# Head norms by transposes and a VectorE sum, and a new order of steps, in a two-layer RWKV-7 and dilated-attention trunk

## The chip, the cores and the metric

One core of a Trainium2 chip runs the whole program. The metric is the device time of one execution in microseconds, the median of several runs. The granted clock of TensorE, which rows below show, has two levels, 1.2 and 2.4 GHz (0.50 and 1.00 in the rows).

## The reference, cut to what matters

The trunk has two layers on 512 positions of width 1024. Each is a feed-forward block, a mixer, and a second feed-forward block. The first mixer is an RWKV-7 scan with 12 heads of 64 plus attention to a memory of 256 rows; the second is dilated attention in 12 heads plus attention to the same memory. The change concerns the norms over the 64 columns of a head:

```python
kk = split_heads(k * kk_scale)
kk = kk / jnp.maximum(jnp.linalg.norm(kk, axis=-1, keepdims=True), 1e-12)   # RWKV keys
...
var = jnp.mean(jnp.square(y - mean), axis=-1, keepdims=True)                # RWKV output
y = ((y - mean) * lax.rsqrt(var + LNX_EPS)).reshape(b, s, RWKV_W) * lnx_g + lnx_b
...
k = rms_norm(split_heads(k), k_gain)        # shared keys of the second mixer
q = rms_norm(q, q_gain)                     # queries of both mixers
```

## The kernel before, in words

Everything is held transposed: a tile `[128, 512]` has two heads of 64 channels on the partitions and the 512 positions along the row. The four feed-forward blocks (tile `fps` in PSUM) and the projections of the mixers (tiles `mm`) multiply in three passes: a value is split into a high and a low part (`uh`, `ul`, `whi`, `wlo`), and each product is three matmuls of 512 columns.

A mixer is a set of generators ("strands"). `weave` runs them in one thread of program order: each letter of `ORDER_A` or `ORDER_B` takes one step of one strand, and a step whose condition doesn't hold yet is owed and taken as soon as it can. In mixer A the letters are a: `finish` (the recurrence and the output norm of a pair of heads), b and c: `scan` of even and odd pairs (the triangular solve), d: `prepare`, e and f: the memory attention of two head pairs, g: the projections, h: the first part of the output projection. In mixer B they are a: memory attention, b and c: dilated attention of even and odd units, d: `settle` (norms of queries and keys, transposes of values), e: projections, f: the first part of the output projection. Each engine works through its own queue in program order.

The norm of a head needs the sum of 64 squares that lie on 64 partitions. ScalarE squares the tile into `sq`. `roots` then takes four blocks of 128 positions as the stationary operand and multiplies each by `pair`, two columns of ones and zeros; the result in a `sc` bank is `[128 positions, 4 blocks, 2 heads]`. VectorE scales it and takes the reciprocal, ScalarE takes the square root, in the wide form spread over 64 columns per head. `spread` brings it back to channels on partitions: four matmuls of 128 columns against the identity, into another `sc` bank, which VectorE multiplies into the tile. Queries of mixer B and of the memory attention need the root by position alone, and use no `spread`.

`roots` is called 14 times in each mixer: in A by `rwkv_prepare` (6), `rwkv_finish` (6) and the memory queries (2), in B for 6 key tiles and 8 query tiles. `spread` is called 12 times in A and 6 times in B. A reader of the profile meets all of this under the line of one recording helper, L309, so that groups are told apart by tile and shape: `sc<-cst,tmp` with `128x2` is `roots`, with `128x128` it is `spread` (and the transposes of values in `settle`).

Of the kernel before, what the change touches and what calls it, by code (L numbers as in the profile page):

```python
# [13 lines left out]
ALU = mybir.AluOpType  # L14
AX = mybir.AxisListType
PSUM = bass.MemoryType.PSUM

P = 128
# [5 lines left out]
HD = 64  # L24
# [143 lines left out]
def wide(t):  # L168
    return t.unsqueeze(1).broadcast_to([P, NCH, C])
# [14 lines left out]
class Operand:  # L184
# [40 lines left out]


ORDER_A = (
    "abcdeaefhhhhhhggggggggfgggggggggggggggggggggggggggggggggggggdddgddggggddddddggdgggggddbbbbbbbggggggb"
    "ddggbbggdbgggggbbgdbdgbbggddddbddggbbggggbggbbgeeeegbdgbbddgaacccaaccaaccgaagaagaacggagaccaaagggaacg"
    "gacchhhhgaaaagcddgdhhhhgccgggcdccdggcggddddddbbccgcggaaaaadcgddgcaggagaaagabbbbbgaaabgaaabbggaabgabg"  # L230
    "ggbgagaaabdbddbgggbgbbddbggddddddbgbbggbbgaadaagaagddgaacaaccaagaagcaaaccggggccaccgacaccggaaaagggcdd"
    "dccgcgccddbbgggcgdddddddccgcggccdgaadaagaagbaabaabbbaagaabgaaabbgaabaggbgggbgagaaagbdddbbgggbdccgbbg"
    "dgbddddddbffcfbbdbbaaddaaaaaacaacccecaaffaacceaaacfcecceeccfaaffecccaeceafaaaacffcchchcahaahaaaahaaa"
    "haaahaaahhaahhaahaahhhhhhhhhhhhhhhhhhhhh"
)
ORDER_B = (
    "ccccabdedfeeeeeeeeeeeeeeeeeeeddddeeddddeeeeeeeeeddddeebbeeebbeeeedaadeedeeddeeeeeddeeeedddeeeeeeedde"
    "edddeeeedeeeeddeeeeedddeeeeeeeedddecceebeeeeeeeeeeeeebddddbbbbbbbceccccccceeeadeedddeffffeeebaaabbee"
    "eeeeeeeacaaaadddcceeeeaedaaeeaeeeedddeeeeeaeaaeddddedddeeedddeeeeeededeedddeeeeeeddeedddbbbbeeeecccc"
    "eedddeeeeeeeeeeeeeeeebdddddcbbbbffccfbbbbcfcccfccffbbffbffcffcc"  # L240
)
WAIT, FREE = "wait", "free"

# [118 lines left out]
class Net:  # L362
# [37 lines left out]
    def load_constants(self):  # L400
        nc = self.nc
        width = self.ap["cst"].shape[1]
        t = self.cp.tile([P, width], F32, name="cst")
        nc.sync.dma_start(t, self.ap["cst"])
        off = 0
        for n, w in zip(CONST_N, CONST_W):
            setattr(self, n, t[:, off:off + w])
            off += w
        self.pair = self.same.rearrange("p (e u) -> p e u", e=2)[:, :, 0]

    def gain(self, i):
        return self.gains[:, i:i + 1]
# [157 lines left out]
    def roots(self, sq, n, bank, wide, keep, *change):  # L570

        nc, nb = self.nc, n // P
        ps = bank("sc")[:, :nb * 2].rearrange("p (b e) -> p b e", e=2)
        for b in range(nb):
            nc.tensor.matmul(ps[:, b], sq[:, b * P:(b + 1) * P], self.pair, start=True, stop=True,
                             skip_group_check=True)
        r = keep or self.cp.tile([P, 4, 2], F32, tag="roots", bufs=2, name=self.nm("roots"))[:, :nb]
        nc.vector.tensor_scalar(r, ps, *change[:2], **{f"op{i}": o for i, o in enumerate(change[2:])})
        nc.vector.reciprocal(r, r)
        yield WAIT  # L580
        if wide:
            w = wide().rearrange("p (b e u) -> p b e u", e=2, u=HD)
            nc.scalar.activation(w, r.unsqueeze(3).broadcast_to([P, nb, 2, HD]), AF.Sqrt)
            r = w.rearrange("p b e u -> p b (e u)")
        else:
            nc.scalar.activation(r, r, AF.Sqrt)
        yield WAIT
        return r

    def spread(self, r, ps):  # L590

        for b in range(r.shape[1]):
            self.nc.tensor.matmul(ps[:, b * P:(b + 1) * P], r[:, b], self.ident, start=True, stop=True,
                                  skip_group_check=True)

    def head_norm(self, out, t, gain, tmp, bank, n, wide=True):

# [761 lines left out]
```

## Time and profile before

| | us |
|---|---|
| median of 3 runs (lowest, highest) | 2098.99 (2094.82, 2103.91) |
| the profiled execution's own time | 2096.68 |
| its span, first to last instruction | 2094.9 |
| TensorE busy in the span | 2049.4 (98%) |
| VectorE, ScalarE, GpSimd busy | 860.6, 817.0, 588.4 |
| mean granted clock of TensorE | 0.992 |

Busy time of TensorE is the union of its matmuls; they are pipelined, so the distance from one start to the next tells more of a matmul's price than its duration. By the tiles, the mixer A has TensorE from 385.5 to 769.2 us of the span and mixer B from 1508.0 to 1729.2 us; the rest are feed-forward blocks.

### The profile page before, as it was taken

The page shows a single profiled execution, that of the slowest core. Times are in us where ns is not written, and L with a number is a line of the kernel's source. Part 1 is how long each engine was busy: PE and PEld are TensorE (multiplying, and loading weights), DVE is VectorE, ACT ScalarE, POOL GpSimd, SP SyncE. Part 2 cuts the span into 40 slices and gives each one's busy share as a digit, 9 for nine tenths or more (in the row PEclk, how much of TensorE's full clock was granted, in tenths as well). Part 3 has the DMA queues.
Part 4 walks back from the last instruction along what each step waited for, and adds up shares of the span by engine and source line. Part 5 has one row for each costly group of instructions (what it writes and reads, how often), then busy time and mean ns, then how long its engine had stood idle before and what let it go on. Part 6 is the DMA issues. An engine that isn't in the chain of part 4 may idle for free.

```text
span 2094.9 us, 35917 instructions
## 1 busy us (share of the span) xinstructions
PE 2049.4 (98%) x14594; PEld 1666.8 (80%) x14594; DVE 860.6 (41%) x1294; ACT 817.0 (39%) x1418; POOL 588.4 (28%) x513
## 2 busy tenths in 40 slices
PE   8999999999998899999999999999999989999999
PEld 6888888877776687788888888888787868888887
DVE  6333333455455355333434433333416375333322
ACT  6333333434334554333433433333336554333321
POOL 2222222553332152222222222222232224222221
PEclk9999999999999999999999999999999999999999
DMA  5333344411100173443344422334521154222342
GB/s 198 96 96 99 93 124 137 124 48 44 36 28 20 45 255 110 135 144 99 110 136 132 146 96 96 100 100 129 157 94 46 43 180 146 95 97 96 99 132 80
DMA packets 130645, 222.13 MB, mean 106 GB/s; under 512 B 14232, under 2 KB 31824, under 8 KB 130480
## 3 DMA queue, kind: packets, MB, share of 16 engines
q1 hardware_dynamic: 130480, 219.85, 33.6%
q8 instruction: 114, 1.87, 0.4%
q14 instruction: 51, 0.42, 0.1%
HBM read 202.90 MB, written 21.61 MB: 107 GB/s over the span
## 4 chain that ended last, share of the span: by engine, by line
PE 71%; DVE 2%; ACT 1%; issue 0%; DMA 0%; ACTq 0%; DVEq 0%
PE fps L309 52%; PE mm L309 10%; PE sc L309 8%; PE py L309 2%; ACT krv L309 0%; DVE prob L309 0%; DVE x L309 0%; DVE mx L309 0%; DVE dmx L309 0%; DVE ul L309 0%; DVE mpr L309 0%; ACT L309 0%; DVE tx L309 0%; ACT tmp L309 0%; DMA xd<-x 0%
## 5 line engine op out<-in xcount | busy, mean ns | idle before, releaser
L309 POOL TENSOR_TENSOR wlo<-raw,whi 128x512 fp32r<-128x512 f32 (+3 forms) x404 | 495.1, 1227 | 1369.8 <-ACT whi L309 1352.7
L309 ACT ACTIVATE whi<-raw 128x512 fp32r<-128x512 f32 (+3 forms) x684 | 415.6, 610 | 935.2 <-PE fps L309 780.2
L309 PE MATMUL fps<-uh,whi 128*128 128x512 f32 x1408 | 551.5, 392 | 8.0 <-ACT whi L309 8.0
L309 PE MATMUL fps<-uh,wlo 128*128 128x512 f32 x1408 | 549.5, 390 | 1.4 <-POOL wlo L309 1.0
L309 PE MATMUL fps<-ul,whi 128*128 128x512 f32 x1408 | 548.9, 390 | 0.0
L309 DVE TENSOR_TENSOR wlo<-raw,whi 128x512 fp32r<-128x512 f32 x280 | 200.8, 718 | 345.1 <-ACT whi L309 335.4
L309 PEld LDWEIGHTS fps<-uh,whi 128*128 128x128 f32 x1408 | 265.0, 188 | 67.5 <-ACT whi L309 12.3
L309 PEld LDWEIGHTS fps<-uh,wlo 128*128 128x128 f32 x1408 | 264.8, 188 | 58.7 <-POOL wlo L309 2.0
L309 PEld LDWEIGHTS fps<-ul,whi 128*128 128x128 f32 x1408 | 264.9, 188 | 55.7 <-issue 0.7
L309 PE MATMUL fps<-hh,whi 128*128 128x512 f32 x704 | 273.9, 389 | 0.0
L309 PE MATMUL fps<-hl,whi 128*128 128x512 f32 x704 | 273.9, 389 | 0.0
L309 PE MATMUL fps<-hh,wlo 128*128 128x512 f32 x704 | 273.9, 389 | 0.0
L309 DVE TENSOR_TENSOR gs<-fps,rstd 128x512 f32<-128x512 f32 x88 | 60.5, 690 | 322.5 <-PE fps L309 322.5
L309 PEld LDWEIGHTS fps<-hl,whi 128*128 128x128 f32 x704 | 132.2, 188 | 27.6
L309 PEld LDWEIGHTS fps<-hh,whi 128*128 128x128 f32 x704 | 132.2, 188 | 27.3
L309 PEld LDWEIGHTS fps<-hh,wlo 128*128 128x128 f32 x704 | 132.2, 188 | 27.3
L309 PE MATMUL mm<-uh,whi 128*128 128x512 f32 x280 | 125.0, 447 | 0.4 <-DVE p L309 0.2
L309 PE MATMUL mm<-uh,wlo 128*128 128x512 f32 x280 | 111.9, 399 | 0.0
L309 PE MATMUL mm<-ul,whi 128*128 128x512 f32 x280 | 111.6, 399 | 0.0
L309 DVE TENSOR_TENSOR hm<-fps,gs 128x512 f32<-128x512 f32 x88 | 60.6, 691 | 121.0 <-PE fps L309 115.8
L309 DVE TENSOR_TENSOR hl<-hm,hh 128x512 fp32r<-128x512 f32 x88 | 77.2, 880 | 50.7 <-ACT hh L309 50.6
L309 PEld LDWEIGHTS mm<-uh,whi 128*128 128x128 f32 x280 | 53.4, 191 | 17.3 <-issue 5.0
(260 smaller groups left out, 2025.6 us busy)
## 6 DMA issues: line engine op xcount, KB each, us to landing
raw<-w SPq DMA_DIRECT2D x512, 256.0 KB, 2.6
raw<-wa_in SPq DMA_DIRECT2D x44, 256.0 KB, 2.7
xd<-x SPq DMA_DIRECT2D x40, 256.0 KB, 3.4
tmp<-xd SPq DMA_DIRECT2D x32, 256.0 KB, 3.2
xin<-xd SPq DMA_DIRECT2D x32, 256.0 KB, 4.4
raw<-w_kv SPq DMA_DIRECT2D x24, 256.0 KB, 2.7
raw<-w SPq DMA_DIRECT2D x32, 128.0 KB, 2.4
raw<-wmem SPq DMA_DIRECT2D x16, 256.0 KB, 2.6
```

The source lines that it names most:

```text
L309: r = f(*args, **kw)
```

## The change

`roots` no longer multiplies the four blocks of squares by two columns. It transposes them on TensorE, so that a `sc` bank holds all 512 squares with positions on the partitions, and VectorE adds up 64 columns per head with a `tensor_reduce` from PSUM. The scaling is then a `tensor_scalar` of its own on the sums in SBUF. `spread` uses transposes in place of matmuls with the identity. `pair` goes. The two order strings are new; they hold the same number of letters of each kind, and the code of the strands is otherwise the same.

```diff
 ORDER_A = (
-    "abcdeaefhhhhhhggggggggfgggggggggggggggggggggggggggggggggggggdddgddggggddddddggdgggggddbbbbbbbggggggb"
...
+    "eeabcdafghhhhghhhhgggggggfgebbbbeeegggggggggggggggggggggggggggggggggggggdddgddggggddddddggbbbdgggggddg"
...
 ORDER_B = (
...
-        self.pair = self.same.rearrange("p (e u) -> p e u", e=2)[:, :, 0]
...
     def roots(self, sq, n, bank, wide, keep, *change):
         nc, nb = self.nc, n // P
-        ps = bank("sc")[:, :nb * 2].rearrange("p (b e) -> p b e", e=2)
+        ps = bank("sc")[:, :n].rearrange("p (b u) -> p b u", u=P)
         for b in range(nb):
-            nc.tensor.matmul(ps[:, b], sq[:, b * P:(b + 1) * P], self.pair, start=True, stop=True,
-                             skip_group_check=True)
+            nc.tensor.transpose(ps[:, b], sq[:, b * P:(b + 1) * P], self.ident)
         r = keep or self.cp.tile([P, 4, 2], F32, tag="roots", bufs=2, name=self.nm("roots"))[:, :nb]
-        nc.vector.tensor_scalar(r, ps, *change[:2], **{f"op{i}": o for i, o in enumerate(change[2:])})
+        nc.vector.tensor_reduce(r, ps.rearrange("p b (e u) -> p b e u", u=HD), axis=AX.X, op=ALU.add)
+        nc.vector.tensor_scalar(r, r, *change[:2], **{f"op{i}": o for i, o in enumerate(change[2:])})
         nc.vector.reciprocal(r, r)
...
     def spread(self, r, ps):
         for b in range(r.shape[1]):
-            self.nc.tensor.matmul(ps[:, b * P:(b + 1) * P], r[:, b], self.ident, start=True, stop=True,
-                                  skip_group_check=True)
+            self.nc.tensor.transpose(ps[:, b * P:(b + 1) * P], r[:, b], self.ident)
```

The new strings move work on every engine. The first place is TensorE in mixer A at the output norm of the fourth of six head pairs (in `finish`): `sc<-cst,tmp` with four matmuls of 2 columns is `roots`, the next `sc<-cst,tmp` is its `spread`, `32x32` are steps of a solve, `mm` is a projection. Before:

```order
L309 MATMUL mm_6800<-uh_2419,wlo_6804 128x512
L309 MATMUL sc_6901<-cst,tmp_6860 128x2 x4
L309 MATMUL sc_6911<-tx_6896,mb_6719 32x32 x32
L309 MATMUL sc_6946<-cst,tmp_6909 128x128 x4
L309 MATMUL mm_6800<-uh_2535,whi_6803 128x512
L309 MATMUL mm_6800<-ul_2536,whi_6803 128x512
```

In the change, TensorE's row from the same `roots` (`sc_6965`) to its `spread` (`sc_7037`) is:

```order
L309 MATMUL sc_6965<-cst,tmp_6889 128x128 x4
L309 MATMUL mm_6975<-uh_2188,whi_6978 128x512
L309 MATMUL mm_6975<-ul_2189,whi_6978 128x512
L309 MATMUL mm_6975<-uh_2188,wlo_6979 128x512
L309 MATMUL sc_6987<-cst,tmp_6985 128x128 x4
L309 MATMUL sc_6998<-TT_6770,tx_6963 32x32 x32
L309 MATMUL mm_6975<-uh_2303,whi_6978 128x512
L309 MATMUL mm_6975<-ul_2304,whi_6978 128x512
L309 MATMUL mm_6975<-uh_2303,wlo_6979 128x512
L309 MATMUL sc_7037<-cst,tmp_6996 128x128 x4
```

One step of a solve stood between the two before; now six matmuls of a projection, another set of transposes (the squares of a memory query) and a step of a solve stand there.

The second place is VectorE's queue at that same norm (`roots_6906` before, `roots_6970` in the change; `TT` and `tx` belong to the solves of two other head pairs). Before:

```order
L309 TENSOR_TENSOR TT_6763<-TT_6763,sc_6862 128x256
L309 STREAM_TRANSPOSE tx_6896<-TT_6763 128x256
L309 TENSOR_SCALAR roots_6906<-sc_6901 128x8
L309 RECIPROCAL roots_6906<-roots_6906 128x8
L309 TENSOR_TENSOR tx_6944<-sc_6911,cst 128x256
```

In the change:

```order
L309 TENSOR_TENSOR tx_6963<-sc_6930,cst 128x256
L309 TENSOR_REDUCE roots_6970<-sc_6965 128x8
L309 TENSOR_SCALAR roots_6970<-roots_6970 128x8
L309 RECIPROCAL roots_6970<-roots_6970 128x8
L309 TENSOR_REDUCE qroots<-sc_6987 128x8
L309 TENSOR_TENSOR ul_8061<-y_3582,uh_8060 128x512
L309 TENSOR_SCALAR qroots<-qroots 128x8
L309 TENSOR_TENSOR TT_6770<-TT_6770,sc_6998 128x256
```

A `TENSOR_REDUCE` stands ahead of each scaling, and the solve's addition to `TT_6770` now has two of them ahead of it.

The third place is TensorE in mixer B where the projections have ended and the second half of the dilated attention begins (`kh,qn` are logits, `cst,prob` transposes of probabilities). Before:

```order
L309 MATMUL sc_16147<-kh,qn_14703 128x512
L309 MATMUL sc_16152<-kh,qn_14705 128x128
L309 MATMUL sc_16153<-kh,qn_14705 128x128
L309 MATMUL sc_16152<-kh,qn_14707 128x128
L309 MATMUL sc_16153<-kh,qn_14707 128x128
L309 MATMUL sc_16172<-cst,prob_16119 128x128 x4
```

In the change:

```order
L309 MATMUL sc_16175<-kh,qn_14717 128x512
L309 MATMUL sc_16180<-kh,qn_14719 128x128
L309 MATMUL sc_16181<-kh,qn_14719 128x128
L309 MATMUL sc_16180<-kh,qn_14721 128x128
L309 MATMUL sc_16181<-kh,qn_14721 128x128
L309 MATMUL sc_16200<-cst,prob_16147 128x128 x4
```

Nothing moved here: no matmul stands between the last logits and the first transposes of probabilities, before or now.

## Rows read from the trace of the kernel before

**Rows 1.** From the profile's page: the span, TensorE's busy time, the chain of work that ended last, by engine, and the loads of weights (count, size, median us from issue to landing).
```profile
span 2094.9 us, 35917 instructions
PE 2049.4 (98%) x14594; PEld 1666.8 (80%) x14594; DVE 860.6 (41%) x1294; ACT 817.0 (39%) x1418; POOL 588.4 (28%) x513
...
PE 71%; DVE 2%; ACT 1%; issue 0%; DMA 0%; ACTq 0%; DVEq 0%
...
raw<-w SPq DMA_DIRECT2D x512, 256.0 KB, 2.6
```

**Rows 2.** Busy time of each engine by stretch: a feed-forward stretch, mixer A, mixer B. Columns: stretch, its length, then busy us of PE, PEld, DVE, ACT and POOL (with instruction counts), granted clock, DMA share, GB/s.
```profile
770.00:1508.00 738.00, 738.00 (x3286) 607.86 (x3285) 285.28 (x374) 270.18 (x442) 179.80 (x145) 1.00 0.39 121
384.10:769.30 385.20, 364.35 (x6798) 281.68 (x6798) 195.60 (x355) 165.56 (x316) 156.25 (x161) 0.97 0.21 66
1508.70:1730.30 221.60, 210.41 (x1243) 168.05 (x1241) 107.92 (x202) 113.80 (x224) 66.53 (x57) 0.98 0.32 101
```

**Rows 3.** TensorE's timeline in mixer B: start us, duration us, instruction. The first block of eight records is a `roots`, the second a `spread`, the block of four is the transposes of a value tile in `settle`.
```profile
1537.00 0.95 PE L309 MATMUL sc<-cst,tmp 128*128 128x2 f32 x8
1537.80 0.49 PE L309 MATMUL mm<-kvh,whi 128*128 128x512 f32 x1
1538.13 0.40 PE L309 MATMUL mm<-kvl,whi 128*128 128x512 f32 x1
1538.36 0.40 PE L309 MATMUL mm<-kvh,wlo 128*128 128x512 f32 x1
...
1539.29 1.05 PE L309 MATMUL sc<-cst,tmp 128*128 128x128 f32 x8
1540.10 0.47 PE L309 MATMUL mm<-kvh,whi 128*128 128x512 f32 x1
1540.41 0.39 PE L309 MATMUL mm<-kvl,whi 128*128 128x512 f32 x1
...
1558.24 0.60 PE L309 MATMUL sc<-cst,tmp 128*128 128x128 f32 x4
1558.60 0.48 PE L309 MATMUL mm<-kvh,whi 128*128 128x512 f32 x1
1558.91 0.40 PE L309 MATMUL mm<-kvl,whi 128*128 128x512 f32 x1
```

**Rows 4.** TensorE's groups by tile and shape over the whole span: count of records, busy us, mean ns of one, idle time before them. The second group holds the `spread`s and 24 transposes of values.
```profile
L309 PE MATMUL sc<-cst,tmp 128*128 128x2 f32 x224 | 27.7, 245 | 2.5 <-ACT tmp L309 2.3 <-DVE TT L309 0.2
L309 PE MATMUL sc<-cst,tmp 128*128 128x128 f32 x168 | 23.4, 279 | 0.8 <-ACT tmp L309 0.5 <-DVE tmp L309 0.3
```

**Rows 5.** VectorE's groups by tile and shape over the whole span, in the same columns: a reduction of a whole PSUM bank (the maximum of the memory attention's logits), and the scaling in `roots` outside the queries.
```profile
L309 DVE TENSOR_REDUCE mx<-sc 128x2 f32<-128x512 f32 x16 | 10.3, 685 | 12.8 <-PE sc L309 12.8
L309 DVE TENSOR_SCALAR roots<-sc 128x8 f32<-128x8 f32 x18 | 3.0, 166 | 34.0 <-PE sc L309 34.0
```

**Rows 6.** Timeline of several engines in mixer A at the place of the first `order` rows above: from a `roots` to its `spread`. In brackets, idle time before the instruction and who ended it.
```profile
635.58 1.01 PE L309 MATMUL sc<-cst,tmp 128*128 128x2 f32 x8
636.52 0.75 PE L309 MATMUL sc<-tx,mb 32*32 32x32 f32 x64
636.63 0.17 DVE L309 TENSOR_SCALAR roots<-sc 128x8 f32<-128x8 f32 x1 [0.83 <-PE sc L309]
636.83 0.20 DVE L309 RECIPROCAL roots<-roots 128x8 f32<-128x8 f32 x1
637.07 0.63 ACT L309 ACTIVATE tmp<-roots 128x512 f32<-128x512 f32 x1 [1.58 <-DVE roots L309]
637.75 1.16 PE L309 MATMUL sc<-cst,tmp 128*128 128x128 f32 x8 [0.47 <-ACT tmp L309]
```

**Rows 7.** Who TensorE waited for, in mixer A (first three rows) and in mixer B (last row): us in total, times, longest.
```profile
PE sc L309 <- ACT tmp L309: 3.5, 4, 1.2
PE py L309 <- ACT H L309: 3.2, 5, 1.5
PE sc L309 <- DVE tx L309: 3.0, 6, 0.8
...
PE sc L309 <- DVE prob L309: 7.8, 4, 6.2
```

**Rows 8.** TensorE's timeline at the third place of the `order` rows, in mixer B.
```profile
1679.24 2.40 PE L309 MATMUL sc<-kh,qn 64*128 64x512 f32 x12 [0.39 <-DVE prob L309]
1687.81 2.79 PE L309 MATMUL sc<-cst,prob 128*128 128x128 f32 x12 [6.17 <-DVE prob L309]
```

**Rows 9.** Busy time by stretch, in the columns of rows 2: the five stretches inside the mixers in which the granted clock is at 0.50, and one that follows the fourth of them.
```profile
421.50:424.90 3.40, 3.40 (x10) 2.67 (x9) 0.12 (x1) 1.96 (x3) 0.83 (x1) 0.50 0.26 77
530.70:541.00 10.30, 10.30 (x84) 6.72 (x88) 1.45 (x2) 3.23 (x8) 2.37 (x3) 0.50 0.10 27
646.80:650.20 3.40, 3.40 (x26) 1.90 (x27) 1.39 (x2) 0.87 (x3) 0.00 (x0) 0.50 0.00 0
677.50:684.30 6.80, 5.57 (x108) 4.22 (x110) 3.27 (x9) 3.08 (x9) 0.92 (x2) 0.50 0.00 0
1684.40:1691.30 6.90, 3.49 (x20) 3.19 (x22) 5.01 (x11) 5.24 (x11) 0.00 (x0) 0.51 0.00 0
685.00:702.00 17.00, 13.96 (x466) 10.33 (x464) 10.45 (x30) 11.92 (x31) 0.00 (x0) 1.00 0.12 35
```

**Rows 10.** One TensorE group in the last of those stretches (685 to 702 us), in the columns of rows 4: transposes of the memory attention's probabilities.
```profile
L309 PE MATMUL sc<-cst,krv 128*128 128x128 f32 x24 | 3.8, 289 | 1.7 <-DVE krv L309 1.3 <-DVE TT L309 0.4
```

More of the change, by code (lines that the diff above doesn't have):

```diff
@@ L227 @@
 ORDER_A = (
-    "abcdeaefhhhhhhggggggggfgggggggggggggggggggggggggggggggggggggdddgddggggddddddggdgggggddbbbbbbbggggggb"
[L229 to L234, printed above, removed]
+    "eeabcdafghhhhghhhhgggggggfgebbbbeeegggggggggggggggggggggggggggggggggggdddgddggggddddddggbbbdgggggddg"
+    "ddgggggbggbbggdbgggbgddbgbggbbggddddbddggbgbgggbggggbbdbhdhghbhbhdhgaacccaacccaagaagaagagcacgffgaacc"
+    "aaagggaacggaccaaaaggcddggdgccggcdccdggcggddddddbbccaaagggcaadcgddgcaggagaaagbbbbbgaabaagabbgagaaabgb"
+    "gggbaaggaaabdbddbgggbgbbddgbgddddddgbbbggbbgaadaagaagddgaacaaccaagagccaaccbbgggagacaccagcaccgagaagag"
+    "gcdddccggcgccdgggcdgdddddddcccggccdgaahhdaagabgaabbgaagbggggbaabaagaaaabbgbagabbgagaaaabdddbggbcgbdg"
+    "bbdgbddddddbbcbcfdbgdbaadaaaacaaaacccecfaaafcaceaaacfcecceeccfaffaecccaeecafaaaaccaaacfcfhchaahaahaa"
+    "ahaaahaaahhhhahhaahaaahhhhhhhhhhhhhhhhhh"
 )
 ORDER_B = (
[L237 to L240, printed above, removed]
+    "eeccfbdfeeefffaeeebbeeeeeeeeeebeeebdccaeddededdeeeeeeeeeeeeeeeddddddddeaeedededdeeeeeddeeedeeddeeeee"
+    "eddeeeeededeededecceddeeeeddedeeeeeeeddeeeeeeeeeeeeeeebbddddebbbbbbdbceeccdeeeeadcdceecdcecebaaabebe"
+    "eeeeeeeacaaaaccbbbbdeeeeeadedeeaadedededeeeadeadeededaadddeeeeedeeeeddddeeeedddeeceeeedeeddddceceece"
+    "ebebeddeeeedeeeeeeebeeebecbfdfddcbdcbdbfbfcccfcfcbfbcffffbffccc"
 )
```

## The prediction

> **What bounds the kernel now.** I read the page first: TensorE is busy for 2049.4 of 2094.9 us, and the chain that ended last lies on it for 71% of the span, with DMA at 0% [rows 1]. Then the stretches: a feed-forward stretch of 738 us has TensorE busy for all of it at clock 1.00, so nothing but fewer matmuls would shorten it, and the change touches none there. The mixers are less full: TensorE idles 385.20 − 364.35 = 20.9 us in mixer A and 221.60 − 210.41 = 11.2 us in mixer B, at clocks of 0.97 and 0.98, while VectorE is busy for about half of each (195.60 and 107.92 us) [rows 2]. So two things set a mixer's time: TensorE's own work, some 95% of it, and a few waits in chains that pass through VectorE and ScalarE [rows 7]. The change takes work from the first and adds to the second.
>
> **What TensorE loses.** Busy time is a poor price for pipelined matmuls, so I take distances between starts, where a block stands among projection matmuls that follow at 0.23 us (1538.13 to 1538.36) [rows 3]. A `roots` of eight records starts at 1537.00 and the second matmul behind it at 1538.13; less one matmul that is 1.13 − 0.23 = 0.90 us. A `spread` takes 1540.41 − 1539.29 − 0.23 = 0.89 us. Two columns cost as much as 128: both are eight records of about 0.11 us. Four transposes, which this kernel already does for values, are four records and take 1558.91 − 1558.24 − 0.23 = 0.44 us [rows 3]. The trace has 224 records of two columns, 28 calls of 8, and 168 − 24 = 144 of `spread`, 18 calls of 8 [rows 4]. Removed: 28 × 0.90 + 18 × 0.89 = 41.2 us. Added: 46 × 0.44 = 20.2 us. **TensorE: −21.0 us**, 11.8 of it in mixer A (26 blocks) and 9.2 in mixer B (20). Bounds: the whole if TensorE is always the limit, and nothing if every block stands ahead of a wait that ends on another engine; the idle shares of 5% say that the first is nearer.
>
> **What VectorE gains in work.** 28 reductions of a PSUM bank. The trace has the same form, 128x512 to a few columns, at 685 ns [rows 5]; 28 × 0.685 = 19.2 us. The scaling stays as one small instruction of 0.17 us. With 9.6 us in each mixer VectorE goes to about 205 of 385 and 118 of 222 us, far from being the bound by its sum. What counts is delay, in two ways.
>
> First, the chain from a `roots` to its `spread`. Where the trace shows it waiting, it takes 637.75 − 635.58 = 2.17 us from first matmul to first matmul; the scaling starts 1.05 us after the first matmul [rows 6]. Now the last of four transposes ends after 0.60 us [rows 3]; with the same 0.04 us to VectorE, 0.69 us of reduction and 0.04 us to the scaling, that is 1.37 us, 0.32 later: 2.49 us. As the block itself occupies TensorE for 0.44 in place of 0.90 us, TensorE needs 2.49 − 0.44 = 2.05 us of other work in between, where it needed 1.27. The new order gives it in most places. In mixer B, six, twelve, six, nine, nine and six projection matmuls stood between; now it is twelve, nine, twelve, fifteen, twelve and six. At 0.23 us each, nine are just enough, and six are 0.68 short, once. In mixer A, the place of the first `order` rows had one solve step (about 0.7 us) and waited 0.47 [rows 6]; now six matmuls, a set of transposes and a step stand there, 2.5 us. Two other places stay short, one with six matmuls (0.68) and one with six and a short step (about 0.33). New waits of 1.7 us less the 0.5 that goes: **+1.2 us**. Lower bound 0, upper bound 18 × 0.78 = 14 us, were all of them as tight as that one.
>
> Second, what is queued behind a reduction: in the second `order` rows a solve's addition to `TT` has two ahead of it, and TensorE waits for that solve's next step. TensorE waits little on VectorE in mixer A (3.0 us for `tx`, the largest) [rows 7]. Bounds: 0, and 19.2 us if each reduction delays TensorE in full; VectorE is idle half the time, so I take a tenth of the upper end: **+1.8 us**.
>
> **What only moves.** Order, weight splits and DMAs: SP's queue is rewritten too, but the chain has no DMA in it [rows 1], so moved loads are hidden behind six buffers of weights; uncovered, a load would cost the 2.6 us from its issue to its landing [rows 1]. Mixer B's large wait of 6.17 us [rows 8] is the softmax of the first dilated unit after the projections, with nothing to put in between; the third `order` rows read the same in both, so it stays. The clock is at 0.50 in five stretches, with TensorE busy for 3.40 + 10.30 + 3.40 + 5.57 + 3.49 = 26.2 us [rows 9]; half of that, some 13 us, would be saved at 2.4 GHz. I assume that the sum of them stays as it is, with 13 us as the bound of a gain.
>
> **Sum.** −21.0 + 1.2 + 1.8 = −18.0 us. The profiled execution took 2096.7 us, so 2078.7; the median of the runs is 2.3 us above that execution, so **2081 us**, with a range of its own of 2074 to 2088.
>
> **A rule that speaks against it.** The rows show transposes in a stretch at full clock: 24 of them between 685 and 702 us, idle time of 3 us among them, with the clock at 1.00 throughout, right after a low stretch [rows 9, 10]. The Trainium skill, "TensorE: Matmul & The Clock Gate", section "Part 4: PE-mode transpose", says that the full clock does not engage for transposes. By that, more low stretches would follow, as in the third rival below; the row of 685 to 702 us does not agree, though matmuls stand between its transposes.
>
> **Rivals.** *Waits take half of it.* The new order is tight elsewhere than the old: reductions sit ahead of the solve's steps, each of which TensorE follows closely. For it: 28 reductions join a queue that runs in program order, waits on `tx`, `H` and `tmp` that already sum to 9.7 us [rows 7]. Doubling these waits gives +9.7 in place of +3.0: 2081 + 7 = 2088, and with mixer B's shortest places up to 2094. Against: covers between `roots` and `spread` grew at the places counted.
>
> *The order also removes low stretches.* The clock fell at 1684.4 while TensorE sat in its wait of 6.17 us [rows 8, 9], so that a better filled row could spare some; if those of mixer A go, 22.7 / 2 = 11 us more: 2070.
>
> *Slower: the clock.* Each short low stretch such as 421.5 to 424.9 costs 3.40 / 2 = 1.7 us [rows 9]. Every one of 46 blocks is now transposes. Eleven more low stretches of that size eat the 18 us, and from seventeen on the kernel is slower by more than 0.5%; were all 46 blocks to bring one, 46 × 1.7 = 78 us, 2159. I give 20 of them as the case: 2081 + 34 = 2115. Against: the stretch of 24 transposes at 1.00, and that TensorE around them is full of projection matmuls.
>
> *No effect.* If the transposes also came as eight records, nothing would be saved and 3 us lost, 2102. The four records of rows 3 say no.
>
> **How the numbers follow.** About 0.5% (10.5 us) is what a measurement of this kernel can tell from no change, so faster means below 2088.5. Chances: the forecast 0.68, half lost to waits 0.15 (a fifth of it still below 2088.5), fewer low stretches 0.08, slower by the clock 0.06, no effect 0.03. Faster: 0.68 + 0.08 + 0.03 = 0.79, which I lower to 0.77 for the tail of the forecast's own range; slower 0.07, of which 0.06 is the clock; the rest, 0.16, is the same. The range leaves out the clock case, no effect and the ends of the others: 2066 to 2095.
>
> **What would show it.** In the profile after: 28 `roots` and 18 `spread` blocks of four records each, 0.44 us from start to start; mixer A shorter by about 10 us and mixer B by about 8, the feed-forward blocks unchanged; VectorE with 28 reductions of about 0.69 us; TensorE's waits for VectorE and ScalarE in the mixers higher by 2 to 4 us; the 6 us wait of mixer B still there. I am wrong if blocks of transposes cost over 0.7 us, if TensorE's idle time in the mixers grows by over 8 us, or if stretches at clock 0.50 sum to over 50 us.

## The result, and the profile after

The median of the changed kernel is 2082.4 us (five runs, 2077.82 to 2083.72), against 2098.99 before: a ratio of 0.9919, with a 95% interval of 0.9903 to 0.9936, which is 17 us less, between 13 and 20. The forecast was 2081. The same kernel, run once more beside other experiments, gave 2081.16, a ratio of 0.9931 (0.9917 to 0.9944), which is 12 to 17 us less. The profiled execution took 2081.52 us in place of 2096.68.

The page of after, against [rows 1] (span, busy time, and the chain that ended last):

```profile
span 2079.6 us, 35581 instructions
...
PE 2029.9 (98%) x14410; PEld 1643.4 (79%) x14410; DVE 882.5 (42%) x1322; ACT 816.3 (39%) x1418; POOL 586.6 (28%) x513
...
PE 68%; DVE 3%; ACT 2%; issue 1%; POOL 0%; DMA 0%; ACTq 0%; DVEq 0%; POOLq 0%
```

TensorE's busy time fell by 2049.4 − 2029.9 = 19.5 us, and its idle time, span less busy, rose from 45.5 to 49.7 us. VectorE gained 21.9 us of work. The chain shows the exchange: three points of a hundred went from TensorE to VectorE, ScalarE and issue.

Busy time by stretch, against [rows 2]: feed-forward, mixer A, mixer B, and then the five stretches inside the mixers with the clock at 0.50, against [rows 9]. Columns: stretch, length, busy us of PE, PEld, DVE, ACT, POOL, granted clock, DMA share, GB/s.

```profile
762.00:1500.00 738.00, 738.00 (x3285) 607.66 (x3284) 286.75 (x375) 269.77 (x443) 179.23 (x145) 1.00 0.40 121
385.10:762.00 376.90, 352.75 (x6685) 268.04 (x6683) 208.65 (x368) 164.61 (x315) 154.57 (x160) 0.96 0.22 67
1501.00:1713.90 212.90, 201.08 (x1163) 157.58 (x1162) 114.66 (x215) 113.41 (x225) 65.00 (x57) 0.98 0.33 104
...
461.40:464.90 3.50, 3.50 (x10) 2.62 (x8) 2.52 (x4) 0.63 (x1) 3.15 (x3) 0.51 0.00 0
529.70:533.10 3.40, 3.40 (x22) 1.98 (x17) 0.69 (x1) 1.25 (x3) 1.28 (x2) 0.50 0.00 0
560.40:567.20 6.80, 6.22 (x75) 5.01 (x75) 5.38 (x9) 1.87 (x4) 2.08 (x3) 0.50 0.00 0
669.60:683.30 13.70, 11.61 (x254) 8.82 (x258) 6.90 (x19) 7.50 (x25) 1.31 (x2) 0.50 0.01 2
1669.80:1676.60 6.80, 4.17 (x26) 3.87 (x28) 4.25 (x8) 4.46 (x9) 0.00 (x0) 0.50 0.01 2
```

From the first projection of each mixer to the first feed-forward matmul behind it, mixer A went from 383.68 us (385.50 to 769.18) to 376.92, and mixer B from 221.13 (1508.04 to 1729.17) to 212.98: 6.8 and 8.1 us less. The feed-forward stretch is the same. TensorE's busy time at half clock is 3.50 + 3.40 + 6.22 + 11.61 + 4.17 = 28.9 us, where it was 26.2.

TensorE's timeline in mixer B, against [rows 3]: a `roots` and the matmuls behind it, and a `spread`. Columns: start us, duration us, instruction. Below them the wait that answers to [rows 8].

```profile
1531.04 0.60 PE L309 MATMUL sc<-cst,tmp 128*128 128x128 f32 x4
1531.40 0.48 PE L309 MATMUL mm<-kvh,whi 128*128 128x512 f32 x1
1531.71 0.40 PE L309 MATMUL mm<-kvl,whi 128*128 128x512 f32 x1
...
1534.94 0.60 PE L309 MATMUL sc<-cst,tmp 128*128 128x128 f32 x4
1535.29 0.47 PE L309 MATMUL mm<-kvh,whi 128*128 128x512 f32 x1
1535.60 0.39 PE L309 MATMUL mm<-kvl,whi 128*128 128x512 f32 x1
...
1672.43 2.79 PE L309 MATMUL sc<-cst,prob 128*128 128x128 f32 x12 [6.17 <-DVE prob L309]
```

Read as in the prediction, the `roots` costs 1531.71 − 1531.04 − 0.23 = 0.44 us and the `spread` 0.43. The wait in mixer B is the same 6.17 us.

Groups of after, against [rows 4] and [rows 5]: instruction, count, busy us, mean ns of one, idle time before.

```profile
L309 PE MATMUL sc<-cst,tmp 128*128 128x128 f32 x208 | 32.7, 281 | 5.2 <-ACT tmp L309 4.7 <-DVE tmp L309 0.3
L309 DVE TENSOR_REDUCE roots<-sc 128x8 f32<-128x512 f32 x18 | 12.4, 687 | 15.1 <-PE sc L309 15.1
L309 DVE TENSOR_REDUCE qroots<-sc 128x8 f32<-128x512 f32 x10 | 6.9, 690 | 5.5 <-PE sc L309 5.5
L309 DVE TENSOR_SCALAR roots<-roots 128x8 f32<-128x8 f32 x18 | 5.0, 278 | 0.5
```

The 208 records are 46 blocks of 4 and the 24 transposes of values. A reduction takes 0.69 us, as assumed. The scaling takes 0.278 us on average where [rows 5] had 0.166; the last section shows why.

Who TensorE waited for in mixer A, against [rows 7] (us in total, times, longest):

```profile
PE sc L309 <- DVE tx L309: 4.6, 7, 2.1
PE sc L309 <- ACT tmp L309: 4.3, 6, 1.7
PE py L309 <- ACT H L309: 3.7, 6, 1.5
...
PE sc L309 <- DVE tmp L309: 3.0, 3, 2.0
```

The three waits that summed to 9.7 us sum to 12.6. The `ACT tmp` row mixes two things: the waits ahead of `roots` fell and those ahead of `spread` rose (the part on why the prediction held tells them apart). At the place of the first `order` rows, where `spread` waited 0.47 us [rows 6], nothing waits now (timeline of several engines in mixer A):

```profile
637.82 0.66 PE L309 MATMUL sc<-cst,tmp 128*128 128x128 f32 x4
638.51 0.69 DVE L309 TENSOR_REDUCE roots<-sc 128x8 f32<-128x512 f32 x1 [0.16 <-PE sc L309]
639.24 0.17 DVE L309 TENSOR_SCALAR roots<-roots 128x8 f32<-128x8 f32 x1
...
641.02 0.60 PE L309 MATMUL sc<-cst,tmp 128*128 128x128 f32 x4
```

The scaling starts 1.42 us after the first transpose (1.37 was worked out), and `spread`, 3.20 us behind, finds its operand ready.

### The profile page after: what moved, and what is told of

It reads as the page before. It is cut to its first block, busy times and chain, and to the rows that moved or that the text cites. A ratio compares the mean times of both kernels' runs of the same rounds, so it can differ in the third digit from the quotient of the medians.

```text
span 2079.6 us, 35581 instructions
## 1 busy us (share of the span) xinstructions
PE 2029.9 (98%) x14410; PEld 1643.4 (79%) x14410; DVE 882.5 (42%) x1322; ACT 816.3 (39%) x1418; POOL 586.6 (28%) x513
## 4 chain that ended last, share of the span: by engine, by line
PE 68%; DVE 3%; ACT 2%; issue 1%; POOL 0%; DMA 0%; ACTq 0%; DVEq 0%; POOLq 0%
PE fps L309 53%; PE mm L309 8%; PE sc L309 6%; PE py L309 2%; DVE tmp L309 1%; ACT L309 0%; DVE prob L309 0%; DVE dmx L309 0%; DVE roots L309 0%; ACT tmp L309 0%; ACT mpr L309 0%; DVE x L309 0%; DMA tmp<-xd 0%; DVE ul L309 0%; ACT prob L309 0%
## 5 line engine op out<-in xcount | busy, mean ns | idle before, releaser
L309 PEld LDWEIGHTS fps<-uh,whi 128*128 128x128 f32 x1408 | 264.8, 188 | 67.4 <-ACT whi L309 11.8
L309 ACT ACTIVATE hh<-hm 128x512 fp32r<-128x512 f32 x88 | 55.2, 631 | 28.6 <-DVE hm L309 28.6
```

The source lines that it names most:

```text
L309: r = f(*args, **kw)
```

## Experiments

The runs of before beside the first four kernels have a median of 2097.41 us (23 runs), beside the next four 2099.22 (11), and beside the last four 2096.84 (9).

**The order without the operations, and the operations without the order.** First kernel: the changed code with both order strings of before.

```diff
 ORDER_A = (
-    "eeabcdafghhhhghhhhgggggggfgebbbbeeegggggggggggggggggggggggggggggggggggggdddgddggggddddddggbbbdgggggddg"
...
+    "abcdeaefhhhhhhggggggggfgggggggggggggggggggggggggggggggggggggdddgddggggddddddggdgggggddbbbbbbbggggggb"
...
```

> The code of the change (transposes, sum on VectorE) with the two order strings of before. Theory (TensorE's work): the 46 blocks still fall from about 0.90 to 0.44 us, so 21 us go; the old order is tighter by about 3 us at the places counted (the 0.47 us wait among them, now longer by 0.78). Time 2080 to 2088, ratio to before 0.991 to 0.995. Rival (the new order is what gains): most of the gain goes with the strings, time over 2091.

Measured: 2092.83 us (11 runs, 2090.8 to 2099.35), ratio 0.9978 (0.9968 to 0.9988). That is 10.4 us above the changed kernel (10 to 12 by the ratios), and only some 5 below before. Mixers A and B by stretch, and below them TensorE's largest waits in mixer A:

```profile
386.20:767.80 381.60, 349.78 (x6685) 265.17 (x6684) 206.26 (x368) 164.28 (x315) 155.37 (x160) 0.98 0.21 66
1506.70:1723.90 217.20, 203.38 (x1164) 158.86 (x1163) 116.74 (x215) 114.61 (x225) 66.30 (x57) 0.98 0.34 102
```

```profile
PE sc L309 <- ACT tmp L309: 7.1, 10, 2.2
PE sc L309 <- DVE tx L309: 5.4, 7, 2.1
PE sc L309 <- issue: 3.7, 5, 1.1
PE py L309 <- ACT H L309: 3.2, 5, 1.5
```

TensorE's idle time is 31.8 us in mixer A and 13.8 in mixer B, where the changed kernel has 24.2 and 11.8: 9.6 us more, about the whole difference. The page gives nearly the same busy time, 2030.6 against 2029.9 us. So in the old order the work does leave TensorE, and 13.5 of its 20.9 us come back as idle time (59.0 us on that page, 45.5 on that of before).

Second kernel: the code of before with both new order strings.

> The code of before (products of two columns, spread by matmuls) with the two new order strings. Theory: no TensorE work goes, so 2099 within 4 us either way. Rival (the order gains): below 2091.

Measured: 2096.6 us (12 runs, 2090.96 to 2099.84), ratio 0.9992 (0.9981 to 1.0003). The new order by itself gives nothing that can be measured, as expected (4 us at most by the interval). The operations alone give about 5 us; together the two give 15 to 17.

**Each of the two edits alone, in the new order.** Third kernel: `roots` transposes and sums, `spread` multiplies as before.

```diff
     def spread(self, r, ps):
         for b in range(r.shape[1]):
-            self.nc.tensor.transpose(ps[:, b * P:(b + 1) * P], r[:, b], self.ident)
+            self.nc.tensor.matmul(ps[:, b * P:(b + 1) * P], r[:, b], self.ident, start=True, stop=True,
+                                  skip_group_check=True)
```

> The change, with spread as matmuls against the identity again: only the squares are turned by transposes and added up by VectorE. Theory: 28 blocks of 0.46 us go, 12.9 us, less some 3 us of waits behind the reductions: 2087 to 2091. Rival (the reductions' delay eats the gain of this half): 2096 or more.

Measured: 2083.7 us (6 runs), ratio 0.9936 (0.992 to 0.9952), 13.4 us less.

Fourth kernel: only `spread` transposes; `roots` is that of before.

> The new orders, spread by transposes, but the sums as products of two columns and no reduction on VectorE. Theory: 18 blocks of 0.45 us go, 8.1 us, and no new wait: 2089 to 2093. Rival (the spread's blocks stand ahead of waits that end elsewhere, so that they are hidden): 2096 or more.

Measured: 2087.61 us (6 runs), ratio 0.9951 (0.9936 to 0.9967), 10.3 us less. TensorE's saving by the block prices is 28 × 0.46 = 12.9 and 18 × 0.45 = 8.1 us, so both gave somewhat more than the whole of it, though the intervals (10 to 17 and 7 to 13 us) hold the whole. Part of that may be the clock: the runs of these two had mean granted clocks of 0.9945 and 0.9938, where those of before and of the changed kernel had 0.993. A thousandth of 2095 us is 2.1 us, and a straight line through the 23 runs of before gives 1.3 us for a thousandth. With 2 to 3 and 1 to 2 us taken off for that, an estimate, they give some 11 and 9, which add up to a little more than the whole, within the intervals. Both medians came out below the 2087 to 2091 and 2089 to 2093 that I expected, so that each edit is worth about its full TensorE time in the new order.

**What the sums cost VectorE.** Fifth kernel: the reduction reads 8 of 64 columns (most of each sum is left out; the transposes stay, and the keys' norm is scaled by 64).

```diff
-        nc.vector.tensor_reduce(r, ps.rearrange("p b (e u) -> p b e u", u=HD), axis=AX.X, op=ALU.add)
+        nc.vector.tensor_reduce(r, ps.rearrange("p b (e u) -> p b e u", u=HD)[:, :, :, :8], axis=AX.X, op=ALU.add)
...
```

> The change, but VectorE adds up 8 of the 64 squares of a head (the norm of the keys is scaled by 64 so that it stays finite), which leaves out most of the sum: the reduction becomes a quarter as long or less, everything else is as in the change. Theory (the reductions cost some 3 us of waits in all): 1 to 4 us below the change, 2078 to 2081. Rival (each reduction delays TensorE in full): 28 x 0.5 = 14 us below it, 2068.

Sixth kernel: the same reduction twice, one behind the other.

> The change with every reduction done twice, 28 more instructions of 0.69 us on VectorE. Theory (VectorE has room, chains have some slack): plus 3 to 8 us, 2085 to 2090. Rival (VectorE's chains are the bound in the mixers): plus 19 us, 2101. Nothing at all would say that the waits of the change are not the reductions' doing.

Measured: 2078.89 us (4 runs, ratio 0.9907, 0.9895 to 0.992) with an eighth of the sum, and 2107.06 (5 runs, ratio 1.0044, 1.0031 to 1.0056) with twice the sum. The group of the fifth, and the stretches of mixers A and B and the largest waits in A of the sixth:

```profile
L309 DVE TENSOR_REDUCE roots<-sc 128x8 f32<-128x64 f32 x18 | 3.9, 219 | 15.5 <-PE sc L309 15.5
```

```profile
385.70:779.00 393.30, 356.93 (x6686) 271.03 (x6685) 214.61 (x382) 164.77 (x315) 155.20 (x160) 0.96 0.20 64
1518.10:1739.50 221.40, 204.13 (x1163) 158.51 (x1162) 129.81 (x229) 113.87 (x225) 65.44 (x57) 0.98 0.32 100
```

```profile
PE sc L309 <- ACT tmp L309: 9.9, 8, 2.3
PE sc L309 <- DVE tx L309: 6.4, 7, 2.1
PE sc L309 <- ACT krv L309: 4.0, 2, 3.5
```

Taking 28 × 0.47 = 13.1 us of reductions from VectorE gives some 2 to 5 us (3.5 and 2.3 by the medians of the changed kernel's two sets of runs, 2.5 and 5.0 by the ratios, and the intervals reach to nothing), and its profiled execution has about the same idle time on TensorE (49.1 us). VectorE's busy time fell by 9.9 us only (882.5 to 872.6): nine scalings now begin inside a GpSimd instruction and last 0.36 to 1.02 us, for which see the last section, so that the run puts the cost of the reductions rather low. Adding 28 × 0.69 = 19.2 us costs 24.7 us. By the pages, of the 25.7 us between the two profiled spans, 17.6 are new idle time of TensorE and 8.1 longer busy time at a lower mean clock (0.989 against 0.992). So most of the first sum lies free under other work, and the same sum a second time is paid in full and more. I expected 3 to 8 us here: I had taken the room on VectorE from its busy share of half, but the room that counts is that between a `roots` and what waits for it. By the timelines, TensorE's waits ahead of a `spread` for ScalarE's root sum to 14.5 us with twice the sum and to 3.7 in the changed kernel, which is 10.8 of the 17.6.

**How much of the old order's loss is the reduction.** Ninth kernel: the old order strings, and the reduction over 8 of 64 columns.

> The transposes with the two order strings of before, as in the first experiment, and VectorE adding up 8 of the 64 squares only (most of the sum is left out). Theory (the old orders give too little work between a roots and its spread, and the reduction is what made that chain longer): most of the 10.4 us that the old orders cost come back, 2092.8 falls to 2083 to 2087. Rival (the old orders are worse for another reason than the reduction): it falls by the 3.5 us that the shorter sum gave with the new orders, to about 2089.

Measured: 2087.78 us (5 runs), ratio 0.9963 (0.995 to 0.9975), and mixer A still idles 29.8 us. By the medians 5.0 of the 10.4 us come back, by the ratios 3.1, where the same edit in the new order gave 2 to 5. The time lies between the two expectations. Set beside the new order it speaks for the rival: with an eighth of the sum the old order is still 8.9 us behind the new one (11.7 by the ratios), with the whole sum 10.4 (10 to 12). So the length of the reduction explains 2 us or less of the old order's loss, which these runs cannot tell from nothing. The loss sits in many waits of 1 to 2 us, `ACT tmp` the first of them (6.3 us, 7 times, where the changed kernel has 4.3). One of them can be read. The longest in the first kernel, 2.15 us, ends at 733.29: there ScalarE loads a table for 1.28 us ahead of its root, from 731.32, when the reciprocal has ended at 730.91. In the changed kernel the same load runs from 728.80, beside the reduction, and the wait is 0.65 us. Which step of the order cures which of the others was not told apart.

**The wait that the change left.** Seventh kernel: the first part of mixer B's output projection waits for six attention units to have begun, instead of for five to be finished.

```diff
                                                            bias[:, 2 * m + e, 7 + g], op0=ALU.mult, op1=ALU.add)
+                    begun.append(unit)
                     yield WAIT
...
-                yield from until(lambda: len(remembered) == 2 and len(finished) >= 5)
+                yield from until(lambda: len(remembered) == 2 and len(begun) >= 6)
```

> The change, but in mixer B the first part of the output projection may begin once the logits of the first two dilated units of the second half are issued, in place of when the fifth unit has ended: projection matmuls then stand where TensorE waits 6.2 us. Theory (that wait is a chain with nothing to put in between, and the low stretch of the clock begins in it): 3 to 6 us faster than the change, 2076 to 2079, and the wait shrinks below 3 us. Rival (the matmuls are missing as cover for the later units): the wait moves, and the time is the same within 2 us.

Measured: 2080.05 us (5 runs, 2076.05 to 2081.16), ratio 0.9907 (0.9893 to 0.9921). TensorE and VectorE at the place of the 6.17 us wait:

```profile
1668.97 0.67 DVE L309 TENSOR_TENSOR x<-mm,tmp 128x512 f32<-128x512 f32 x1
1669.57 1.74 DVE L309 TENSOR_REDUCE dmx<-prob 128x2 f32<-128x1536 f32 x1
1671.30 0.66 DVE L309 TENSOR_TENSOR x<-mm,tmp 128x512 f32<-128x512 f32 x1
1671.88 1.13 DVE L309 TENSOR_SCALAR prob<-prob,dsm 128x768 f32<-128x768 f32 x2
...
1672.63 2.79 PE L309 MATMUL sc<-cst,prob 128*128 128x128 f32 x12 [4.37 <-DVE prob L309]
```

Twelve projection matmuls, some 2.7 us, now run ahead of the wait, but it shrinks by 1.8 us only, to 4.37: each projection ends in an addition on VectorE (`x<-mm,tmp`), and two of these stand ahead of the scaling of `prob` for which TensorE waits. I had counted TensorE's side and left out what the moved work queues on VectorE. The time lies above the 2076 to 2079 that I expected, and its interval overlaps that of the changed kernel, so it isn't shown to be faster.

Tenth kernel: the same, and three more steps of that projection drawn ahead in `ORDER_B`.

```diff
-    "ebebeddeeeedeeeeeeebeeebecbfdfddcbdcbdbfbfcccfcfcbfbcffffbffccc"
+    "ebebeddfffeeeedeeeeeeebeeebecbfdfddcbdcbdbfbfcccfcfcbfbcfbffccc"
```

> The earlier start of the output projection, with three more of its steps drawn ahead into the wait of mixer B (nine more projection matmuls, 2.1 us). Theory: the wait of 4.4 us falls to about 2.5, and the time by 1 to 2 us below 2080. Rival (the nine matmuls are missing as cover for the last two units, and additions of finished columns stand ahead of the softmax on VectorE): the same within 1.5 us, or slower.

> The change itself once more, beside the others on one chip: 2079 to 2084, and a mean granted clock that goes with the time from run to run.

Measured: 2080.93 us (5 runs), ratio 0.9927 (0.9915 to 0.994), beside 2081.16 (0.9931, 0.9917 to 0.9944) for the changed kernel run with it: the same. The wait stayed at 4.38 us, where I expected 2.5: as in the seventh kernel, twelve projection matmuls run ahead of it, so the moved steps did not come to stand there. No version here is shown to beat the changed kernel.

**Transposes, two columns, and the clock.** Two probes on the changed kernel, each in the feed-forward stretch: eighth kernel, 200 transposes of 128x128 in a row; twelfth, 100 matmuls of two columns (200 records).

```diff
+            if which == "01":
+                pr = bank().rearrange("p (b u) -> p b u", u=P)
+                for i in range(200):
+                    nc.tensor.transpose(pr[:, i % 4], self.ident, self.ident)
...
```

> The change, with 200 transposes of the identity in a row ahead of the second product of the second feed-forward block. At 0.11 us each they take 22 us, so about 2104 in all. Theory (transposes hold the clock as matmuls do): granted clock 1.00 through the row, pitch 0.11 us. Rival (the skill's rule that the full clock does not engage for transposes): the clock falls to 0.50 within the row and the pitch doubles, so 35 to 45 us for the row and 2115 or more in all.

> The change, with 100 matmuls of the identity by two columns in a row where the transposes alone stood. Theory (a product of two columns pays for two loads of 128x128 weights): 200 records at 0.11 us, 22 us, 2104 in all, as long as the 200 transposes. Rival (so few columns cost less outside a mixer): under 12 us, 2094.

Measured: 2105.46 and 2119.92 us (one run each). First the stretch and the group of the row of transposes, then the stretches (the clock is the third figure from the end) and the group of the row of two columns:

```profile
1022.20:1043.90 21.70, 21.70 (x200) 21.68 (x199) 1.59 (x2) 1.27 (x2) 1.28 (x1) 1.00 0.08 23
```

```profile
L309 PE MATMUL fps<-cst 128*128 128x128 f32 x200 | 22.0, 273 | 0.0
```

```profile
1018.00:1023.10 5.10, 5.10 (x48) 5.10 (x46) 1.58 (x2) 1.26 (x2) 1.27 (x1) 1.00 0.32 95
1023.10:1055.70 32.60, 32.60 (x155) 32.60 (x154) 0.00 (x0) 0.00 (x0) 0.00 (x0) 0.50 0.00 1
```

```profile
L309 PE MATMUL fps<-cst 128*128 128x2 f32 x200 | 38.0, 329 | 0.0
```

The transposes come at 21.7 / 200 = 0.109 us each with the clock at 2.4 GHz throughout. The two-column products start at the same pitch, 5.1 / 47 = 0.109 us (one of the 48 records is a matmul ahead of the row); then the clock falls to 1.2 GHz, though TensorE was busy without a gap, and the pitch is 0.21 us to the end of the row. That is why the row took 38 us and not the 22 that I expected, and the run 2120 us and not 2104; at 2.4 GHz a two-column product did cost as much as two transposes. The rule of the Trainium skill ("TensorE: Matmul & The Clock Gate", "Part 4: PE-mode transpose") that the full clock does not engage for transposes is not borne out by the row of transposes. It began at the full clock, so it shows that 21.7 us of transposes did not lose it, and not whether transposes would raise it from 1.2 GHz.

## Why the prediction held, point by point

**TensorE: −21.0 us.** Right. Busy time fell by 19.5 us; busy time at half clock grew by 28.9 − 26.2 = 2.7 us, half of which, 1.4, is the clock's doing. At equal clock that is −20.9 us.

**Waits: +1.2 and +1.8 us.** The sum is right in size, a little low: TensorE's idle time rose by 4.2 us (2 to 4 was the forecast, 3.0 the sum): 3.3 in mixer A, 1.1 in mixer B, and 0.2 less elsewhere. The first of the two terms is not right. TensorE's waits ahead of a `spread` for ScalarE's root were 0.5 us before and are 3.7 now, at five places, where three places and 1.7 us were forecast. Two of the three came out (0.62 us in mixer B and 0.65 in A, for 0.68); the third waits 1.67 us for 0.33, and two more wait 0.24 and 0.48. TensorE and ScalarE at the third, in mixer A:

```profile
555.93 0.66 PE L309 MATMUL sc<-cst,tmp 128*128 128x128 f32 x4
559.00 1.28 ACT L309 ACT_TABLE_LOAD   x1 [3.03 <-DVE roots L309]
560.98 1.11 PE L309 MATMUL sc<-cst,tmp 128*128 128x128 f32 x4 [1.67 <-ACT tmp L309]
```

From first matmul to first matmul that is 5.05 us, not 2.49. ScalarE loads a table for 1.28 us ahead of its root, and the scaling lasts 1.09 us (last section). The chain of [rows 6], from which 2.49 was worked out, has no such load; in the trace of before, six of the twelve chains in mixer A have one behind the reciprocal, at this place from 562.27 to 563.55. The two places that were not forecast have both a load and a long scaling. That the sum of the waits still came out near is partly luck: the waits ahead of `roots` fell from 2.5 to 1.2 us, which was not forecast. The sum with an eighth of the columns gave 2 to 5 us back, so the reductions themselves delay little.

**The clock: 0.** It cost 1.4 us in the profiled execution. With that, −20.9 + 4.2 + 1.4 = −15.3 us, the difference of the spans, for −18.0 forecast. The profiled execution took 2.8 us more than the 2078.7 that were worked out for it. That the median came within 1.4 us of the forecast is luck in part: it lies 0.9 us above the profiled execution, where 2.3 were added.

**Mixers A and B: −10 and −8 us.** B came out right, at −8.1. A came out at −6.8: the waits in A were put some 1.5 us too low, and 1 us went to the clock (24.7 us busy at half clock in A, 22.7 before). The mis-sized step is the wait term: one measured chain was taken as the length of all of them, and the rest was a tenth of an upper bound.

**The order: part of a term of +1.2 us.** Here the reason was thinner than the number. I used the new order to count the covers, and the counts were right (12, 9, 12, 15, 12 and 6 matmuls in mixer B), but treated it as a detail that lowers a small term. The runs show that the same code in the old order loses 10 to 12 us of its 15 to 17, nearly all to idle time of TensorE. My own bounds held this case: nothing to 14 us ahead of the `spread`s, nothing to 19.2 us behind the reductions. In the old order the waits ahead of a `spread` sum to 6.4 us, 6.0 more than before, and the other 7.5 of the 13.5 us of new idle time lie elsewhere. I did not work that out, and for the first kernel I expected 2080 to 2088, 5 us too low at its upper end.

**The rivals.** Waits did not take half: idle rose by 4.2 us, not 10. In the old order they take 13.5 of 20.9. The clock: five low stretches as before, 28.9 us in place of 26.2, and a row of transposes alone at full clock. No effect is out by the 0.44 us blocks, and the order did not remove low stretches.

**VectorE far from the bound by its sum.** True of the sum, misleading as a reason. Busy for 55% of mixer A, it still has no room for a second reduction, as the sixth kernel shows.

## What to carry to other kernels

An edit that shortens one engine's work and lengthens a chain on another is worth its full price only if the program order around it leaves the new chain its time, so price edit and order together, and try each without the other before calling either useless. Take an engine's room not from its busy share but from the gap between an instruction's operands and the first reader of its result, and test it by doubling the instruction. Follow each chain in the trace by itself: a length measured at one place does not hold where a table load or a wait for another engine stands in the chain. When work is moved into a wait, count what it queues on the engine that is waited for.

## What the runs showed of the hardware

**A scaling in SBUF waits for GpSimd.** Of 28 scalings after, five are longer than 0.17 us (0.27, 0.41, 0.45, 0.55, 1.09), and each of the five starts inside a GpSimd instruction and ends 0.02 to 0.03 us behind it. GpSimd and VectorE in mixer A, first the longest after, then a scaling of before:

```profile
557.40 1.26 POOL L309 TENSOR_TENSOR inv<-TT,cst 128x512 f32<-128x512 f32 x1
557.59 1.09 DVE L309 TENSOR_SCALAR roots<-roots 128x8 f32<-128x8 f32 x1
...
607.07 1.28 POOL L309 TENSOR_TENSOR inv<-TT,cst 128x512 f32<-128x512 f32 x1 [0.21 <-DVE TT L309]
607.54 0.17 DVE L309 TENSOR_SCALAR roots<-sc 128x8 f32<-128x8 f32 x1 [0.56 <-PE sc L309]
```

The first two end at 558.66 and 558.68. Before, the same scaling read the sums from PSUM and took 0.17 us also in the middle of a GpSimd instruction (607.54, inside one from 607.07 to 608.35). The reciprocal, which works from SBUF to SBUF, was not held: 0.20 us at 558.72, inside the next GpSimd instruction. The five cost 1.9 us on VectorE, and three of them stand in chains that TensorE waits for (422.64, 560.98 and 653.15). The Trainium skill ("SBUF — State Buffer", "Who interferes with whom") has the rule: a `tensor_scalar` in a two-port mode and GpSimd exclude each other for a whole instruction, and a `tensor_reduce` doesn't take part. The trace agrees with the first half by the five scalings, and nothing in it speaks against the second: the reduction at 606.33, inside a GpSimd instruction from 606.25 to 607.55, took 0.69 us as the others did. The reductions here read PSUM, so no row shows one from SBUF. The prediction priced the scaling at an unchanged 0.17 us, with the row of a scaling that read PSUM. A version that scales elsewhere was not run.

**Two rows and the clock.** In one run each, a row of 200 records of two-column products fell to 1.2 GHz after 5.1 us while TensorE was without a gap, and a row of 200 transposes stayed at 2.4 GHz for its 21.7 us, at the same pitch at first. Why was not tested.

**The clock from run to run.** The 23 runs of before beside the first four kernels have mean granted clocks of 0.990 to 0.996, and times from 2102 down to 2092 us, which fall as the clock rises, though not run by run (at 0.995 from 2093.9 to 2097.8). A gain of a few us in one profiled execution can go with the clock.
